# Two-layer streaming-encoder trunk on one core: second-matrix pairs with eight of sixteen row tiles in seven products, in single rotating rooms

## The chip, the cores and the metric

The kernel runs on one core of a Trainium2 chip. The core has a matrix engine (TensorE, in the profile PE, with its weight loads as PEld), a vector engine (DVE), a scalar engine (ACT), GpSimd (POOL) and SyncE (SP), which issues most of the DMA transfers. Each engine works through its own list of instructions in order and waits on semaphores for the others. The metric is the device time of one execution in microseconds, as the median of several runs.

## The reference

The input is a sequence of 256 rows of 2048 floats, batch 1. The model has two layers; what matters here are the two MLPs, one at the end of each layer:

```
def sq_relu_mlp(h, g, w1, w2):
    a = jax.nn.relu(rms_norm(h, g) @ w1)      # w1: 2048 x 8192
    return (a * a) @ w2                       # w2: 8192 x 2048

layer 1: h = h + attention_a(h) @ a_w_out;  h = h + sq_relu_mlp(h, ...)
shared:  k, v = split(rms_norm(h) @ kv_w)
layer 2: h = h + attention_b(h, k, v) @ b_w_out;  h = h + sq_relu_mlp(h, ...)
```

All values are float32. Both attentions have 16 heads of 128. The output is the 256 x 2048 result of the second layer.

## The kernel before, in words

**Products.** Every float32 operand is split into a high part `hi`, which the matrix engine can take at speed, and a low part `lo`, the remainder. A product is three passes (`passes`, lines 465 to 475): high by high, low activations by high weights, high activations by low weights. The activations are the stationary operand (128 x 128), the weights the moving one (128 x 512). The weights come from HBM; `issue` (lines 205 to 226) lets ACT copy a tile into `hi` (line 219) and DVE subtract to get `lo` (line 220). Each tile has 1024 columns, that is two blocks of 512. The `hi` and `lo` tiles have three buffers each, tiles of 512 columns (`hih`, `loh`) one.

**Pairs.** The output columns of a matrix are worked in panels of 512, two panels to a *pair*, a (first panel) and b (second). A pair has sixteen row tiles of 128 to sum over. A plain unit, written a4 or b7, takes two row tiles of one panel: 12 matmuls. Some of the row tiles go through seven products instead of eight (the Strassen-Winograd scheme on a 2 x 2 split of weights and rows). With weight blocks called 11, 12, 21 and 22, the sums T1 = 12 + 11, T3 = 22 + 12, T2 = T3 + 11 and T4 = T2 + 21 are made, and the seven *forms* use, in this order, 11, T3, T2, T1, 21, T4, 22 (numbers 0 to 6). The matching sums of activations are tiles `S` (from the normalised input) or `Sh` (from the hidden values), made by `sums` (lines 277 to 297). A plain pair has four row tiles in the seven products, a *wide* pair six: each of its forms has 1536 columns, a first half f of 1024 columns (6 matmuls) and a second half h of 512 (3 matmuls). After the second half of form 1, ACT copies an accumulator to the tile P7 (line 908) and puts a negated copy of another in its place (line 914); after that of form 2, DVE subtracts P7 (line 910); later line 918 adds it.

**The MLP.** The 8192 hidden columns are worked in four chunks c of 2048. Each chunk has two pairs of the first matrix, then two pairs of the second, which add to the residual stream. All second-matrix pairs (16 in the kernel, 8 in each MLP) and all but the first of the first-matrix pairs are wide. The hidden values of a chunk come in four quarters n of 512, one for each panel of the two first-matrix pairs. `turn_hidden` (lines 866 to 879) transposes a finished quarter in 32 x 32 blocks on DVE (line 331), carries it through HBM (`carry`: rows out at line 341, columns in at line 347) and then, in `take` (lines 842 to 864), applies relu (line 843), square into the high part (line 848), square (line 850) and the low part (line 854); the first two quarters also make `Sh`. Row tiles 8 to 11 are the third quarter (n = 2), 12 to 15 the fourth (n = 3).

**What sets the order.** `Pair.plan` (lines 130 to 142) writes the order of a pair's units by hand. A wide pair starts f0 h0 b5 f1 h1 b6 f2 h2 b7 f3 h3, where b5 to b7 are the last three units of the pair before; then its own a3 f4 h4 b3 f5 h5 a4 f6 h6 b4 a5 a6 a7. The loop in `mlp` (lines 898 to 930) takes the units one after another. For a plain unit `fetch` first calls `top_up`, which splits units ahead until three full ones are ready, and takes the first. A form's half is taken without topping up if one is ready; after a second half `top_up(AHEAD - 1)` splits until two full ones are ready, and the copy of line 908 stands ahead of that call. A ready tile with fewer than 1024 columns is not counted (line 233). After each plain unit `run_fill` takes one step off the list of side work (the steps of `carry` and `take` among it, at the numbers in `uses`, line 875). `keep_order` holds DVE, ACT, PE and SP to the order in which the program writes their instructions.

**Rooms.** The four blocks of a pair are loaded by SP (`bring`, line 811) into tiles with the tags `k` (blocks 11 and 22) and `v` (12 and 21), each with two buffers of 1536 columns. T3 is made by DVE (line 824) in a room called `bias`; T2 replaces T3 in place once T3 is split (line 224). T1 and T4 are made by POOL (`put`, line 830): a DMA that adds block 11 from HBM onto the room of 12, or block 21 onto the room of T2. `prepare` (lines 832 to 835) does this for the next pair when a given number of plain units is left before it, by the tuple `close = (7, 5, 1, 4, 3, 2)` for 12, 22, 21, 11, T3, T1.

Of the kernel before, what the change touches and what calls it, by code (L numbers as in the profile page):

```python
# [9 lines left out]
F32 = mybir.dt.float32  # L10
# [22 lines left out]
WIDE = UN + 512  # L33
WIDE1 = (1, 2, 3, 4, 5, 6, 7)
# [15 lines left out]
def trunk(ctx: ExitStack, tc: tile.TileContext, xT, xr, gs, hg, bf, wgate, w_in, w_oa, w1a, w1fa, w1sa, w2fa, w2sa,  # L50
# [24 lines left out]
    def load_x(i):  # L75
        raw_x[i] = qkv.tile([P, WIDE], F32, name="xin", tag="kv"[i // 2], bufs=2)[:, : GH * T].rearrange("p (a t) -> p a t", a=GH)
        if i:
            SY.dma_start(raw_x[i], xT[:, i * GH : (i + 1) * GH, :])
# [40 lines left out]
    class Pair:  # L119
# [3 lines left out]
        def __init__(self, big, src, order, third, units, wide=False):  # L123
            self.big, self.src, self.third, self.units, self.order = big, src, third, units, order
            self.ps, self.t, self.adds, self.wide, self.own = None, {}, order != "early", wide, 3 if wide else 2
# [4 lines left out]
        def plan(self, rest):  # L130
            made = [self.items(f"f{i} h{i}" if self.wide else f"f{i}") for i in range(7)]
            own = {"early": "a2 F a3 F b2 F b3 a4 b4 a5 a6 a7", "wide": "a3 F b3 F a4 F b4 a5 a6 a7", "ahead": "a3 F a4 F a5 F a6 a7 b3 b4",
                   "query": "a2 F b2 F a3 F b3 a4 b4 a5 a6 a7", "": "a2 F a3 F a4 F a5 a6 a7 b2 b3 b4"}[self.order].split()
            plan = made[0] + rest[:1] + made[1] + rest[1:2] + made[2] + rest[2:] + made[3]
            n = 4
            for i in own:
                if i == "F":
                    plan += made[n]
                    n += 1
                else:  # L140
                    plan += self.items(i)
            return plan, self.items("b5 b6 b7")

    def plan_mlp(w1, w1f, w1s, w2f, w2s, tail, more=None):
        pairs = []

        def add(w, wf, ws, i, wides, order, when):
            j = wides.index(i) if i in wides else i - sum(1 for k in wides if k < i)
            names = ("11", "12", "21", "22")
            if i in wides:  # L150
                src = [[None] * 3 + [ws[10 * j + 5 * q + u] for u in range(5)] for q in range(2)]
# [4 lines left out]
            pairs.append(Pair(big, src, order, len(pairs) % 2 == 0, when, i in wides))  # L156
# [48 lines left out]
    def issue(parts=1):  # L205
        form = None
        if not raws:
            load(parts)
        raw, cuts = raws.popleft()
        if not cuts:  # L210
            form, half = raw, raw.half
            raw, cuts = form.pair.t[form.name], [slice(0, 512 if half else UN)]
            if half:
                raw = raw[:, UN:]
        n = cuts[-1].stop
        hi = wsp.tile([P, n], F32R, name="hi" if n == UN else "hih", bufs=3 if n == UN else 1)
        lo = wsp.tile([P, n], F32R, name="lo" if n == UN else "loh", bufs=3 if n == UN else 1)
        for c in cuts:
            S.activation(hi[:, c], raw[:, c], AF.Copy)  # L219
            V.tensor_tensor(lo[:, c], raw[:, c], hi[:, c].bitcast(F32), op=ALU.subtract)  # L220
# [136 lines left out]
    def query_room(i):  # L357

        if not query:
            query.append(prob.tile([P, 9 * 3 * P], F32, name="query", tag="p", bufs=1))  # L360
        return query[0][:, i * UN : i * UN + UN]


    LONG = ((0, 0, 1, 3, 5, 6, 7, 8, 8), (0, 1, 2, 4, 6, 7), (0, 0, 1, 3, 5, 6), (0, 0, 1, 3, 5, 6))
# [133 lines left out]
    def form_products(ps, hi, lo, x, fs, i, half, stop):  # L498
        items = []
        for g in (2,) if half else range(2):  # L500
            if i in (0, 4, 5):
                xp = [x[2 * g + (i > 0)][:, k, (i == 5) * P : (i == 5) * P + P] for k in range(2)]
            else:
                c = {3: 0, 2: 1, 1: 2, 6: 3}[i]
                c = c * P if half else c * 256 + g * P
                xp = [fs[k + 2 * half][:, c : c + P] for k in range(2)]
            items.append((ps[i not in (4, 5)][i in (0, 5)], xp, g % 2, i < 2 and g == 0, i < 2 and g == stop))
# [87 lines left out]
    class Rooms:  # L595
# [3 lines left out]
        def open(self):  # L599
            self.t = prob.tile([P, 9 * 3 * P], F32, name="pbuf", tag="p", bufs=1)  # L600
            self.n = dict.fromkeys(self.at, 0)
# [174 lines left out]
    def decay_bias(g, box):  # L776
        nb = room("bias", "nb").rearrange("p (a t) -> p a t", a=GH)
# [12 lines left out]
    for g in range(NG):  # L790
# [12 lines left out]
        zk, k = turned(), room("k", "k")[:, : GH * T]  # L803
        v = room("v", "v")[:, :UN].rearrange("p (b c) -> p b c", b=NB)
# [8 lines left out]
    def make(p, name):  # L813
        t = p.t
        if name == "T3":
            if p.order in ("query", ""):
                t[name] = query_room(0)
            else:
                t[name] = prob.tile([P, 9 * 3 * P], F32, name="wT3", tag="p", bufs=1) if p.order == "early" else room("bias", "wT3")
# [3 lines left out]
        d, a, b = (t[i][:, : WIDE if p.wide else UN] for i in (name, a, b))  # L823
        V.tensor_tensor(d, a, b, op=ALU.add)

    def put(p, name):
# [3 lines left out]
        G.dma_start(p.t[name][:, : WIDE if p.wide else UN], p.big[other], accum_op=ALU.add)  # L830

    def prepare(p, d):
        for name, at in zip(("12", "22", "21", "11", "T3", "T1"), p.units):
            if d == at:
                (bring if name[0] != "T" else put if p.adds and name == "T1" else make)(p, name)

    def mlp(plan, x, Sx, st, last, more=None):
# [4 lines left out]
        def take(t, c, n):  # L842
# [16 lines left out]
            if n == 0:  # L859
                r = prob.tile([P, 9 * 3 * P], F32R, name="Sh", tag="p", bufs=1)  # L860
                Sh[c].extend(r[:, i : i + n] for i, n in ((0, UN), (UN, UN), (2 * UN, 512), (2 * UN + 512, 512)))
# [36 lines left out]
        for i, (p, q, u) in enumerate(plan):  # L898
# [5 lines left out]
            if q > 1:  # L904
                form_products(p.ps, hi, lo, p.x, p.fs, u, q == 3, 1 + p.wide)
# [5 lines left out]
                if q == 2 + p.wide:  # L911
                    top_up(AHEAD - 1)
                    if u == 1:
                        S.activation(p.ps[1][0], p.ps[1][1], AF.Copy, scale=-1.0)
            else:
# [49 lines left out]
    def rel_bias(g, box):  # L965
        rb = room("bias", "rb").rearrange("p (a t) -> p a t", a=GH)
# [11 lines left out]
    for g in range(NG):  # L978
        zk, k = turned(), room("k", "k")[:, : GH * T]
        v = room("v", "v")[:, :UN].rearrange("p (b c) -> p b c", b=NB)  # L980
# [30 lines left out]
def _wide(w):  # L1011

    import numpy as np
    c, n = w.shape[0] // D, w.shape[1] // 1024
    a = w.reshape(c, KT, P, n, 2, 512).transpose(0, 3, 4, 1, 2, 5)
    f = a[:, :, :, :6].reshape(c, n, 2, 3, 2, P, 512).transpose(0, 1, 4, 2, 5, 3, 6)
    s = a[:, :, :, 6:].reshape(c, n, 2, 5, 2, P, 512).transpose(0, 1, 2, 3, 5, 4, 6)
    return np.ascontiguousarray(f).reshape(-1, P, WIDE), np.ascontiguousarray(s).reshape(-1, P, UN)


def _pairs(w, wides):
# [3 lines left out]
    f, s = _wide(w)  # L1025
    f, s = f.reshape(-1, 4, P, WIDE), s.reshape(-1, 10, P, UN)
# [54 lines left out]
```

## Time and profile before

| what | us |
|---|---|
| median of 3 runs (2085.22 to 2088.07) | 2087.54 |
| the profiled execution: span from first to last instruction | 2084.3 |
| busy PE / DVE / ACT / POOL in that span | 2076.9 / 1629.7 / 1256.1 / 118.4 |
| one second-matrix pair, from 623.09 to 664.57 of the span | 41.48 |

The profile gives one execution, whose own time is its span; the median of the runs shown lies 3.2 us above it. Its parts are: busy time by engine; the span in 40 slices with the granted clock of the matrix engine (full speed in all 40); DMA queues; the chain of work that ended last, followed back from the last instruction; the costliest groups of instructions; and DMA issues with the time from issue to landing. A timeline row gives the start, the duration, the engine, the line of the kernel, the operation, the tiles written and read with their shapes, the count, and in brackets the engine's idle time before it with what ended it. Busy time is not a bound by itself: matmuls overlap, and an engine that is often idle can still be late at one place.

### The profile page before, as it was taken

Reading aid. Unit: us, or ns where it says so; the run is one execution under the profiler, and the core shown is the slowest. Engines: PE = TensorE matmul, PEld = TensorE weight load, DVE = VectorE, ACT = ScalarE, POOL = GpSimd, SP = SyncE. Lnnn points to the kernel's source line nnn. Section 1 sums busy time; section 2 is a strip of 40 time slices with the busy share of each in tenths; the row PEclk is TensorE's granted clock in tenths of the full one; section 3 lists DMA queues with packets and bytes.
Section 4 is the critical chain, followed back from the end, with each engine's and each line's share of the span. In section 5 each row is a group of like instructions: output and inputs, shape, how many; then the busy total and the mean of one; then the engine's idle time right before and its main releaser. Section 6 shows DMA issues by size and latency. Waiting matters only on the chain.

```text
span 2084.3 us, 26346 instructions
## 1 busy us (share of the span) xinstructions
PE 2076.9 (100%) x9230; PEld 1721.4 (83%) x9230; DVE 1629.7 (78%) x1964; ACT 1256.1 (60%) x1637; POOL 118.4 (6%) x131
## 2 busy tenths in 40 slices
PE   9999999999999999999999999999999999999999
PEld 7888888888888888888878888888888888888887
DVE  6767666888788888788888677778987887888786
ACT  6544455766566566567676455456765665665664
POOL 1111000000000000000011001000000000000000
PEclk9999999999999999999999999999999999999999
DMA  7787788798798799789988777787987987988895
GB/s 288 247 257 243 225 258 265 253 276 277 235 286 270 251 278 298 217 276 294 269 244 276 225 239 234 244 265 265 282 264 254 278 272 241 289 271 250 271 288 165
DMA packets 181397, 540.93 MB, mean 260 GB/s; under 512 B 36864, under 2 KB 71568, under 8 KB 181264
## 3 DMA queue, kind: packets, MB, share of 16 engines
q1 hardware_dynamic: 170384, 483.60, 68.7%
q0 software_dynamic: 10592, 55.08, 14.3%
q8 instruction: 72, 1.18, 0.2%
q10 hardware_dynamic: 288, 0.57, 0.1%
q14 instruction: 61, 0.50, 0.1%
HBM read 499.30 MB, written 39.87 MB: 259 GB/s over the span
## 4 chain that ended last, share of the span: by engine, by line
PE 98%; DMA 1%; DVE 0%; ACT 0%; issue 0%; ACTq 0%; DVEq 0%; SPq 0%
PE acc L473 26%; PE acc L471 26%; PE acc L475 26%; PE s L471 6%; PE s L473 6%; PE s L475 6%; PE s L614 1%; PE po L644 1%; DMA w<-in_w2fa 0%; PE s L613 0%; PE po L645 0%; DMA raw<-in_w_in 0%; DVE lo L220 0%; ACT hi L219 0%; PE s L737 0%
## 5 line engine op out<-in xcount | busy, mean ns | idle before, releaser
L220 DVE TENSOR_TENSOR lo<-raw,hi 128x1024 fp32r<-128x1024 f32 (+1 forms) x574 | 695.5, 1215 | 219.5 <-ACT hi L219 203.6
L219 ACT ACTIVATE hi<-raw 128x1024 fp32r<-128x1024 f32 (+1 forms) x574 | 602.8, 1051 | 255.6 <-PE acc L473 194.8
L471 PE MATMUL acc<-hi,act 128*128 128x512 f32 x2108 | 580.3, 393 | 1.6 <-ACT hi L219 1.6
L473 PE MATMUL acc<-hi,act 128*128 128x512 f32 x2108 | 571.3, 389 | 0.1
L475 PE MATMUL acc<-lo,act 128*128 128x512 f32 x2108 | 570.9, 389 | 0.0
L473 PEld LDWEIGHTS acc<-hi,act 128*128 128x128 f32 x2108 | 395.5, 188 | 83.2 <-DVE act L311 0.7
L475 PEld LDWEIGHTS acc<-lo,act 128*128 128x128 f32 x2108 | 395.6, 188 | 82.2
L471 PEld LDWEIGHTS acc<-hi,act 128*128 128x128 f32 x2108 | 393.7, 188 | 81.5 <-ACT hi L219 1.7
L219 ACT ACTIVATE hi<-w 128x1024 fp32r<-128x1024 f32 x138 | 145.7, 1056 | 108.1 <-DMA w<-in_w1fa 25.1
L220 DVE TENSOR_TENSOR lo<-w,hi 128x1024 fp32r<-128x1024 f32 x138 | 167.5, 1214 | 27.4 <-ACT hi L219 25.0
L220 DVE TENSOR_TENSOR lo<-wT,hi 128x1024 fp32r<-128x1024 f32 x94 | 114.6, 1219 | 64.0 <-ACT hi L219 64.0
L219 ACT ACTIVATE hih<-w 128x512 fp32r<-128x512 f32 x120 | 75.2, 627 | 76.5 <-PE acc L473 65.5
L219 ACT ACTIVATE hi<-wT 128x1024 fp32r<-128x1024 f32 x94 | 99.1, 1055 | 27.7 <-PE acc L473 9.1
L471 PE MATMUL s<-hi,act 128*128 128x512 f32 x386 | 104.6, 389 | 0.0
L475 PE MATMUL s<-lo,act 128*128 128x512 f32 x386 | 104.6, 389 | 0.0
L473 PE MATMUL s<-hi,act 128*128 128x512 f32 x386 | 104.6, 389 | 0.0
L219 ACT ACTIVATE hih<-wT 128x512 fp32r<-128x512 f32 x90 | 56.4, 627 | 72.9 <-PE acc L473 63.2
L220 DVE TENSOR_TENSOR loh<-w,hih 128x512 fp32r<-128x512 f32 x120 | 82.3, 686 | 18.9 <-ACT hih L219 18.8
L473 PEld LDWEIGHTS s<-hi,act 128*128 128x128 f32 x386 | 72.5, 188 | 15.1
L475 PEld LDWEIGHTS s<-lo,act 128*128 128x128 f32 x386 | 72.5, 188 | 15.0
L471 PEld LDWEIGHTS s<-hi,act 128*128 128x128 f32 x386 | 72.4, 188 | 15.0
L220 DVE TENSOR_TENSOR loh<-wT,hih 128x512 fp32r<-128x512 f32 x90 | 62.0, 689 | 21.0 <-ACT hih L219 20.7
(220 smaller groups left out, 1961.4 us busy)
## 6 DMA issues: line engine op xcount, KB each, us to landing
raw<-in_w_in SPq DMA_DIRECT2D x95, 512.0 KB, 4.5
raw<-in_w2sa SPq DMA_DIRECT2D x80, 512.0 KB, 5.8
raw<-in_w2sb SPq DMA_DIRECT2D x80, 512.0 KB, 5.8
raw<-in_w1sa SPq DMA_DIRECT2D x70, 512.0 KB, 6.0
raw<-in_w1sb SPq DMA_DIRECT2D x70, 512.0 KB, 6.0
raw<-in_w_kv SPq DMA_DIRECT2D x64, 512.0 KB, 4.5
turn<-z SPq DMA_DIRECT2D x60, 512.0 KB, 4.2
w<-in_w2fa SPq DMA_DIRECT2D x32, 768.0 KB, 7.4
```

Of the source, the lines that this page charges most:

```text
L219: S.activation(hi[:, c], raw[:, c], AF.Copy)
L220: V.tensor_tensor(lo[:, c], raw[:, c], hi[:, c].bitcast(F32), op=ALU.subtract)
L471: TE.matmul(ps[:, cols], xh, cut(hi, j), start=first, stop=False, **kw)
L473: TE.matmul(ps[:, cols], xl, cut(hi, j), start=False, stop=False, **kw)
L475: TE.matmul(ps[:, cols], xh, cut(lo, j), start=False, stop=last, **kw)
L614: TE.matmul(s[:, P : 3 * P], q[:, a, P:T], k[:, a], start=True, stop=True)
L644: TE.matmul(po[:, :T], v[:, 0, a * P : (a + 1) * P], pT[:, :2], start=True, stop=False)
```

## The change

The second-matrix pairs become *deep*: eight of the sixteen row tiles go through the seven products. Each form has 2048 columns, in two halves of 1024 (6 matmuls each), and eight plain units are left. The order of a deep pair's own units after h3 is a4 f4 h4 b4 f5 h5 a5 f6 h6 a6 a7. T3 is made in two halves, the first where T3 was made, the second one plain unit later; T2 is made in two halves, each after the matching half of T3 is split. The sums `Sh` of the second hidden quarter have twice the size. After each second half of a deep form `run_fill` is called as well, and the `uses` of the third and fourth quarters get other numbers.

The tags `k` and `v` with two buffers each become four tags `k0`, `k1`, `v0`, `v1` with one buffer each of 2048 columns, and so does `bias`. Which block goes to which tag rotates from pair to pair: 12 takes the room that 11 had, 22 that of 12, 11 that of 21, 21 that of 22. The tile of the pool `prob` grows from 3456 to 4096 columns, and the on-chip space for software DMA descriptors is set to 2048 bytes.

The diff, cut to its core (the host-side layout of the weights and the renaming of widths are left out):

```diff
+DEEP = 2 * UN
...
-        def __init__(self, big, src, order, third, units, wide=False):
+        def __init__(self, big, src, order, third, units, wide=UN):
...
+            self.deep, self.wide = wide == DEEP, wide > UN
+            self.cols, self.own = wide, wide // 512
...
-            own = {... "wide": "a3 F b3 F a4 F b4 a5 a6 a7", ...
+            own = {... "wide": "a3 F b3 F a4 F b4 a5 a6 a7", "deep": "a4 F b4 F a5 F a6 a7", ...
...
+        rooms = {"12": "v0", "22": "k0", "11": "k1", "21": "v1"}
...
-                add(None, w2f, w2s, i, WIDE2, "wide", close)
+                add(None, w2f, w2s, i, WIDE2, "deep", close, DEEP)
...
         for p in pairs:
+            p.rooms = rooms
+            if p.adds:
+                rooms = {"12": rooms["11"], "22": rooms["12"], "11": rooms["21"], "21": rooms["22"]}
...
-            raw, cuts = form.pair.t[form.name], [slice(0, 512 if half else UN)]
+            raw, cuts = form.pair.t[form.name], [slice(0, form.pair.cols - UN if half else UN)]
...
-        if form and half == form.pair.wide:
+        if form and form.pair.deep and form.name == "T3":
+            make(form.pair, "T2", int(half))
+        elif form and half == form.pair.wide:
...
     def half_next():
         u = raws[0][0] if raws else units[0]
-        return isinstance(u, Form) and u.half
+        return isinstance(u, Form) and u.half and not u.pair.deep
...
-        return qkv.tile([P, WIDE], dtype, name=name, tag=tag, bufs=1 if tag == "bias" else 2)
+        return qkv.tile([P, DEEP], dtype, name=name, tag=tag, bufs=1)
...
-    LONG = ((0, 0, 1, 3, 5, 6, 7, 8, 8), (0, 1, 2, 4, 6, 7), ...
+    LONG = ((0, 0, 1, 3, 10, 11, 12, 13, 13), (0, 1, 2, 4, 8, 9), ...
...
-        for g in (2,) if half else range(2):
+        groups = p.cols // 512
+        for g in range(2, groups) if half else range(2):
...
-        p.t[name] = room("kv"[name in ("12", "21")], "w" + name)
-        SY.dma_start(p.t[name][:, : WIDE if p.wide else UN], p.big[name])
+        p.t[name] = room(p.rooms[name], "w" + name)
+        SY.dma_start(p.t[name][:, : p.cols], p.big[name])
...
-        d, a, b = (t[i][:, : WIDE if p.wide else UN] for i in (name, a, b))
+        cols = slice(0, p.cols) if half is None else slice(half * UN, min(half * UN + UN, p.cols))
+        d, a, b = (t[i][:, cols] for i in (name, a, b))
...
-        G.dma_start(p.t[name][:, : WIDE if p.wide else UN], p.big[other], accum_op=ALU.add)
+        G.dma_start(p.t[name][:, : p.cols], p.big[other], accum_op=ALU.add)
...
     def prepare(p, d):
+        if p.deep and d == p.units[4] - 1:
+            make(p, "T3", 1)
         for name, at in zip(("12", "22", "21", "11", "T3", "T1"), p.units):
-            if d == at:
+            if d == at and p.deep and name == "T3":
+                make(p, "T3", 0)
+            elif d == at:
                 (bring if name[0] != "T" else put if p.adds and name == "T1" else make)(p, name)
...
             elif n == 1:
-                yield from sums([[t3[:, 2 * j + b : 2 * j + b + 1] for j in range(2)] for b in range(NB)], Sh[c][2:], 1)
+                yield from sums([[t3[:, 2 * j + b :: 4] for j in range(2)] for b in range(NB)], Sh[c][2:])
...
-                    uses = ((4, 5, 6, 7, 8, 9, 9), (4, 5, 5, 5, 6, 7, 7), (4, 5, 6, 7), (4, 4, 5, 5))[n]
+                    uses = ((4, 5, 6, 7, 8, 9, 9), (4, 5, 5, 5, 6, 7, 7), (6, 7, 8, 9), (6, 6, 7, 7))[n]
+                    wait = int(n == 3)
...
-                    add_fill(carry(*zt, 0)[:2] + [[step] * uses.count(i) for i in range(3, uses[-1] + 1)])
+                    add_fill(carry(*zt, wait)[: 2 + wait] + [[step] * uses.count(i) for i in range(3 + wait, uses[-1] + 1)])
...
                 if q == 2 + p.wide:
                     top_up(AHEAD - 1)
                     if u == 1:
                         S.activation(p.ps[1][0], p.ps[1][1], AF.Copy, scale=-1.0)
+                    if p.deep:
+                        run_fill()
...
-    nc = bacc.Bacc("TRN2", target_bir_lowering=False, num_devices=1)
+    nc = bacc.Bacc("TRN2", target_bir_lowering=False, num_devices=1, dynamic_dma_scratch_size=2048)
```

More of the change, by code (lines that the diff above doesn't have):

```diff
@@ L121, in trunk @@
         fast = True
-        def __init__(self, big, src, order, third, units, wide=False):
-            self.big, self.src, self.third, self.units, self.order = big, src, third, units, order
-            self.ps, self.t, self.adds, self.wide, self.own = None, {}, order != "early", wide, 3 if wide else 2
+        def __init__(self, big, src, order, third, units, wide=UN):
+            self.big, self.src, self.third, self.units = big, src, third, units
+            self.ps, self.t, self.adds, self.order = None, {}, order != "early", order
+            self.deep, self.wide = wide == DEEP, wide > UN
+            self.cols, self.own = wide, wide // 512
         def items(self, names):
@@ L145, in plan_mlp, with add @@
         pairs = []
-        def add(w, wf, ws, i, wides, order, when):
+        def add(w, wf, ws, i, wides, order, when, cols=WIDE):
             j = wides.index(i) if i in wides else i - sum(1 for k in wides if k < i)
@@ L155, in add @@
                 big = {k: src[int(k[1]) - 1][int(k[0]) - 1] for k in names}
-            pairs.append(Pair(big, src, order, len(pairs) % 2 == 0, when, i in wides))
+            pairs.append(Pair(big, src, order, len(pairs) % 2 == 0, when, cols if i in wides else UN))
         close = (7, 5, 1, 4, 3, 2)
+        rooms = {"12": "v0", "22": "k0", "11": "k1", "21": "v1"}
         for c in range(NCH):
@@ L504, in form_products @@
                 c = {3: 0, 2: 1, 1: 2, 6: 3}[i]
-                c = c * P if half else c * 256 + g * P
+                c = c * P if half and not p.deep else c * 256 + g % 2 * P
                 xp = [fs[k + 2 * half][:, c : c + P] for k in range(2)]
-            items.append((ps[i not in (4, 5)][i in (0, 5)], xp, g % 2, i < 2 and g == 0, i < 2 and g == stop))
+            items.append((ps[i not in (4, 5)][i in (0, 5)], xp, g % 2, i < 2 and g == 0, i < 2 and g == groups - 1))
         passes(items, hi, lo, skip_group_check=True)
@@ L818, in make @@
             else:
-                t[name] = prob.tile([P, 9 * 3 * P], F32, name="wT3", tag="p", bufs=1) if p.order == "early" else room("bias", "wT3")
+                t[name] = prob.tile([P, 4 * UN], F32, name="wT3", tag="p", bufs=1) if p.order == "early" else room("bias", "wT3")
         else:
@@ L904, in mlp @@
             if q > 1:
[L905 removed]
+                form_products(p.ps, hi, lo, p.x, p.fs, u, q == 3, p)
                 if u == 1 and q == 2 + p.wide:
```

56 lines of the change are left out of this document (30 added, 26 removed).

## The prediction

> **What bounds the kernel now.** I read the engines' shares first, then the chain that ended last, then the windows of the changed stage, then the timelines of one pair.
>
> ```profile
> span 2084.3 us, 26346 instructions
> ...
> PE 2076.9 (100%) x9230; PEld 1721.4 (83%) x9230; DVE 1629.7 (78%) x1964; ACT 1256.1 (60%) x1637; POOL 118.4 (6%) x131
> ...
> PE 98%; DMA 1%; DVE 0%; ACT 0%; issue 0%; ACTq 0%; DVEq 0%; SPq 0%
> ```
>
> TensorE sets the end: 98% of the chain. The next rows are two windows, the two second-matrix pairs of one column chunk (I call them pair 0 and pair 1).
>
> ```profile
> 623.09:664.57 41.48, 41.48 (x184) 34.36 (x183) 35.52 (x39) 29.32 (x35) 1.71 (x2) 1.00 1.00 303
> 664.57:706.05 41.48, 41.48 (x184) 34.36 (x183) 31.09 (x32) 22.81 (x28) 1.71 (x2) 1.00 0.77 239
> ```
>
> Columns: busy us of PE, PEld, DVE, ACT, POOL, then granted clock, DMA share, GB/s. A pair's plan has 7 first halves of 6 matmuls, 7 second halves of 3 and 10 units of 12: 183. 41.48 / 183 = 0.2267 us each, without a hole, although DVE is only 75 to 86% busy. So matmuls removed here are time gained, if the engines that feed PE keep the order that hides them. I write f0 to f6 and h0 to h6 for a form's halves, a4, b7 and so on for plain units; a pair starts f0 h0 b5 f1 h1 b6 f2 h2 b7 f3 h3.
>
> **What is removed.** A deep pair has 14 halves of 6 matmuls and 8 units of 12: 180. Three fewer in 16 pairs: 48 x 0.2267 = **-10.9 us**.
>
> **What is moved: the units behind the halves.** `top_up` counts a tile shorter than 1024 columns as nothing. A wide second half was such a tile, so two full units stood ready behind it. A deep second half is full: `fetch` at b5 stops at b5, f1, h1, and when h1 has been taken nothing is left. b6 is then split after h1's products, in ACT's written order after the copy P7 (line 908), which waits for h1 on PE. Before, b6's split came first (first row, line 219; it ends 626.69):
>
> ```profile
> 625.64 1.05 ACT L219 ACTIVATE hi<-raw 128x1024 fp32r<-128x1024 f32 x1
> 630.09 0.60 ACT L908 ACTIVATE p<-s 128x512 f32<-128x512 f32 x1 [3.40 <-PE s L475]
> 630.59 1.05 ACT L219 ACTIVATE hi<-wT 128x1024 fp32r<-128x1024 f32 x1
> 631.53 0.59 ACT L914 ACTIVATE s<-s 128x512 f32<-128x512 f32 x1
> ```
>
> ```profile
> 629.66 0.39 PE L475 MATMUL s<-loh,Sh 128*128 128x512 f32 x1
> 629.89 1.07 PE L471 MATMUL acc<-hi,act 128*128 128x512 f32 x4
> 630.80 1.07 PE L473 MATMUL acc<-hi,act 128*128 128x512 f32 x4
> 631.71 1.07 PE L475 MATMUL acc<-lo,act 128*128 128x512 f32 x4
> 632.61 0.62 PE L471 MATMUL s<-hi,Sh 128*128 128x512 f32 x2
> ```
>
> 629.66 is h1's last matmul, 629.89 b6's first, 632.61 f2's first: b6 hides the chain from P7 to f2, whose `hi` is ready at 631.64, only 0.97 us before it is wanted. In the changed kernel the split at 630.59 is b6's own. PE, free at 629.89, stands until 631.64, plus about 0.03 for the signal: 1.78 us. Queued behind P7 on ACT are both splits and the copy of line 914. **16 x 1.78 = +28.5 us.**
>
> **The same drain on DVE after h2.** Line 910 waits for h2; the low part of b7, before it in the order until now, comes after it.
>
> ```profile
> 634.42 0.39 PE L475 MATMUL s<-loh,Sh 128*128 128x512 f32 x1
> 634.65 1.07 PE L471 MATMUL acc<-hi,act 128*128 128x512 f32 x4
> ```
>
> ```profile
> 633.65 1.23 DVE L220 TENSOR_TENSOR lo<-raw,hi 128x1024 fp32r<-128x1024 f32 x1 [0.15 <-ACT hi L219]
> 634.85 0.70 DVE L910 SCALAR_TENSOR_TENSOR acc<-s,p 128x512 f32<-128x512 f32 x1
> 635.54 1.23 DVE L220 TENSOR_TENSOR lo<-w,hi 128x1024 fp32r<-128x1024 f32 x1
> 638.42 1.31 DVE L331 STREAM_TRANSPOSE z<-acc 128x512 f32<-128x512 f32 x2
> 639.65 1.18 DVE L220 TENSOR_TENSOR lo<-w,hi 128x1024 fp32r<-128x1024 f32 x1
> 646.90 1.22 DVE L854 TENSOR_TENSOR act<-q,act 128x1024 fp32r<-128x1024 f32 x1
> 648.04 1.22 DVE L220 TENSOR_TENSOR lo<-w,hi 128x1024 fp32r<-128x1024 f32 x1
> ```
>
> Line 910 starts 0.20 after h2 (634.85 against 634.65) and hands over after 0.69. b7's low part then ends at 0.20 + 0.69 + 1.22 + 0.03 = 2.14, and b7's third pass wants it at 8 x 0.2267 = 1.81: 0.33 in every pair. In pair 0 the queue goes on: low parts of f3 and h3, the two transposes of the last hidden quarter, low parts of a4 and f4, and behind them line 854 for the third hidden quarter, which `run_fill` at h3 now puts directly ahead of a4, its first reader. Full operations follow each other at 1.14 (646.90 to 648.04), the transposes take 1.23 (638.42 to 639.65). From h2's end: 0.20 + 0.69 + 3 x 1.14 + 1.23 + 2 x 1.14 + 1.22 + 0.03 = 9.07. PE asks for it in a4's second pass: b7 2.72, f3 and h3 2.72, first pass 0.91, in all 6.35. Wait 2.72, with the 0.33 in it. In pair 1 line 592 stands for the transposes and nothing of line 854: no more than the 0.33. **8 x 2.72 + 8 x 0.33 = +24.4 us** (ends: 16 x 0.33 = 5.3 if the queue has a hole for line 854, and 24.4).
>
> **The fourth hidden quarter, pair 0.** Its steps move to a5 and h6; a6 reads it.
>
> ```profile
> 652.56 0.61 PE L475 MATMUL s<-lo,Sh 128*128 128x512 f32 x2
> ```
>
> ```profile
> 652.76 1.06 ACT L219 ACTIVATE hi<-raw 128x1024 fp32r<-128x1024 f32 x1 [0.75 <-PE s L473]
> 653.73 1.04 ACT L843 ACTIVATE q<-q 128x1024 f32<-128x1024 f32 x1
> ```
>
> With three `hi` buffers a split starts 0.20 after the second pass of the unit three places before (652.76 against 652.56). Line 854 is written behind the splits of a6 and a7, and a7 waits for f6. From a5's start: f6's second pass ends at 2.72 + 0.91 = 3.63; a7's `hi` ends at 3.83 + 1.05 = 4.88, its low part hands over 1.17 later, line 854 ends at 7.27 + 0.03. a6's second pass would come at 2.72 + 2 x 1.36 + 0.91 = 6.35. 0.95 late: **8 x 0.95 = +7.6 us** (ends 0 and 7.6).
>
> **The start of pair 0.** T3 becomes two halves, the second ahead of h0's low part, and the sums of lines 286 to 289 double.
>
> ```profile
> 619.53 1.06 ACT L219 ACTIVATE hi<-w 128x1024 fp32r<-128x1024 f32 x1 [2.16 <-DMA w<-in_w2fa]
> ```
>
> ```profile
> 610.18 0.42 DVE L286 TENSOR_TENSOR sum<-q 128x256 f32<-128x256 f32 x1
> 611.65 2.35 DVE L220 TENSOR_TENSOR lo<-raw,hi 128x1024 fp32r<-128x1024 f32 x2
> 613.92 1.28 DVE L296 TENSOR_TENSOR Sh<-sum,Sh 128x512 fp32r<-128x512 f32 x2
> 619.78 1.71 DVE L824 TENSOR_TENSOR wT<-w,w 128x1536 f32<-128x1536 f32 x1
> 621.42 1.21 DVE L220 TENSOR_TENSOR lo<-w,hi 128x1024 fp32r<-128x1024 f32 x1
> ```
>
> ```profile
> raw<-in_w2sa SPq DMA_DIRECT2D x80, 512.0 KB, 5.8
> w<-in_w2fa SPq DMA_DIRECT2D x32, 768.0 KB, 7.4
> wT<-in_w2fa POOLq DMA_DIRECT2D x8, 768.0 KB, 7.5
> w<-in_w2fa POOLq DMA_DIRECT2D x8, 768.0 KB, 8.9
> ```
>
> DVE's run from f0's low part to h1's: f0 1.14, four sums 1.47 (610.18 to 611.65), T3's second half 1.14, h0 1.14, two lines 296 1.28, b5 and f1 2.28, T2's first half 1.14, h1 1.22: 10.8 us. PE wants the end at 623.09 + 3 x 1.36 + 2.72 + 0.91 = 630.80. With a T3 half of 1.14 for the 1.64 of 619.78, DVE is free at 620.9: ends 631.7, 0.9 late. But f0's `hi` waits at 619.53 for a load that grows from 768 to 1024 KB: by the rows at 512 and 768, 1.6 us more. Then f0's low part starts at 619.53 + 1.6 + 1.06 = 622.2 and the run ends 2.2 late. I take 1.6: **8 x 1.6 = +12.8 us** (ends 7 and 18).
>
> **Costed at nothing.** The accumulates T4 and T1 grow to 1 MB, by the same step some 9 and 11 us; T4 is asked for after eight units (h2 to b4, 5 x 1.36 + 3 x 2.72 = 15 us), T1 after 19; if that cover goes, ACT's `hi` waits for the DMA and each us costs PE 16. A pair moves 10 MB for 9.5; the DMA share is 1.00 in pair 0, but the waits stretch that window. The free order of the four rooms lets loads start earlier; no matmul here waits for a room, so nothing is gained. No row shows a smaller descriptor scratch (2048 bytes): 0, else as T4's delay.
>
> **Sum.** -10.9 + 28.5 + 24.4 + 7.6 + 12.8 = +62.4. The profiled span 2084.3 becomes 2146.7; the median, 3.2 us above that span, 2087.5 + 62.4 = **2149.9 us**, 3.0% slower.
>
> **The rivals.**
> 1. *Faster.* If b6's split stands before P7 on ACT, as at 625.64, and the low parts likewise, PE never waits and the gain is kept: 2076.6. The point that decides is whether a fourth unit is ready at h1. For it: DVE's 25% of idle time. Against: the written order, which idle time does not change. Chance 0.10.
> 2. *Only the two copies' waits*, 28.5 and 16 x 0.33, because these very waits let DVE catch up elsewhere: -10.9 + 33.8, 2110.4. For it: DVE idles while PE waits; against: the queue behind line 910 starts after that idle time. Chance 0.25.
> 3. *Transfers late too.* The share of 1.00 says pair 0's window is near full; T1 or T4 2 us late in each pair adds 32: 2182. Against: 15 us of cover. Chance 0.10.
> 4. *The clock falls* at the waits. PE's idle time before its first real matmul left it alone:
>
> ```profile
> 7.20 0.73 PE L471 MATMUL acc<-hi,act 128*128 128x512 f32 x2 [1.55 <-ACT hi L219]
> ```
>
> The clock is 1.00 in every window, and 1.55 us did not change that; waits up to 2.7 are not shown. If one 2.72 us unit ran at half speed after each P7 wait, 16 x 2.72 = 43.5 more: 2193. Chance 0.03. The Trainium skill ("TensorE: Matmul & The Clock Gate", HAM oscillation) puts the gap that throttles at about 3.4 us, by which nothing is added, and the row of 1.55 agrees; its section on psum-queue depth-cycling says that frequent short idling throttles too, which would be this rival.
>
> My forecast has 0.52: 2150, its own bounds 2123 (line 854 on time everywhere: 8 x 2.39 + 7.6 less) to 2155 (the start 2.2 late). The range takes in rival 2 and some of rival 3: 2105 to 2172, about 8 in 10. 0.2% (4 us) is about what a measurement of this kernel can tell from no change: faster 0.10, same 0.02, slower 0.88.
>
> **What would show it.** PE holes of 1.8 us before the first matmul of a unit behind each h1 with ACT's line 908 in front of its `hi`; in pair 0 a hole inside a4 ended by line 854; matmuls 9182. No hole at all, or holes ended by DMA, would prove me wrong.

## The result, and the profile after

The changed kernel takes 2174.26 us (2172.68 to 2184.92) against 2087.14 for the kernel before beside it: a ratio of 1.0425, interval 1.0407 to 1.0442. It is 87.1 us slower; I had forecast 62.4 more, with an upper end of 2172. The profiled execution is the slowest of the six, 2184.92 where the others lie between 2172.68 and 2177.02, so its count of what the clock does, below, is that of a slow one.

The page of the kernel after, in the rows that answer to those of before:

```profile
span 2183.1 us, 26253 instructions
...
PE 2105.0 (96%) x9182; PEld 1719.0 (79%) x9182; DVE 1683.2 (77%) x1972; ACT 1287.5 (59%) x1613; POOL 117.9 (5%) x131
...
PE 3%; ACT 0%; issue 0%; DVE 0%; DVEq 0%; ACTq 0%
...
w<-in_w2fa SPq DMA_DIRECT2D x32, 1024.0 KB, 7.9
```

9182 matmuls are the 48 fewer that were forecast. The chain's shares add up to 3%: it was followed back only a little way, so nothing can be read from it, and the windows and timelines have to do. The two pairs of one chunk in the kernel after (PE, PEld, DVE, ACT, POOL busy, granted clock, DMA share, GB/s):

```profile
458.95:510.03 51.08, 44.33 (x182) 34.39 (x180) 41.24 (x42) 31.96 (x35) 2.53 (x3) 0.97 0.86 270
510.03:553.21 43.18, 41.45 (x181) 33.63 (x180) 34.62 (x33) 25.05 (x27) 1.72 (x2) 1.00 0.70 200
```

180 matmuls need 40.8 us. Pair 1 lost 2.4 and pair 0 lost 10.3, where the forecast had 2.1 (1.78 + 0.33) and 7.1 (1.78 + 2.72 + 0.95 + 1.6). Some 1.7 of pair 0's 10.3 is the clock, shown below. The DMA share did not rise to the limit: 0.86, less than the 1.00 of before. Pair 0's timeline shows where; TensorE first:

```profile
463.45 0.73 PE L485 MATMUL s<-lo,act 128*128 128x512 f32 x2 [2.04 <-DVE lo L228]
469.32 0.73 PE L485 MATMUL s<-lo,Sh 128*128 128x512 f32 x2
471.69 1.47 PE L481 MATMUL acc<-hi,act 128*128 128x512 f32 x4 [1.63 <-ACT hi L227]
487.85 1.20 PE L483 MATMUL acc<-hi,act 128*128 128x512 f32 x4 [2.04 <-DVE act L872]
```

The idle time in brackets runs from the modelled end of a matmul; a matmul's slot is shorter. h1's last two start at 469.32, so b6 could have started at 469.32 + 2 x 0.2267 = 469.77 and started at 471.69: 1.91 lost where the bracket has 1.63. I add these 0.28 to each bracket: the third pass of h0 (463.45) lost 2.3, the second of a4 (487.85) also 2.3. What ACT and DVE did meanwhile:

```profile
457.34 2.01 ACT L227 ACTIVATE hi<-w 128x1024 fp32r<-128x1024 f32 x2 [3.81 <-DMA w<-in_w2fa]
470.09 0.60 ACT L927 ACTIVATE p<-s 128x512 f32<-128x512 f32 x1 [5.46 <-PE s L485]
470.59 1.05 ACT L227 ACTIVATE hi<-raw 128x1024 fp32r<-128x1024 f32 x1
```

```profile
458.43 1.23 DVE L228 TENSOR_TENSOR lo<-w,hi 128x1024 fp32r<-128x1024 f32 x1 [1.31 <-ACT hi L227]
459.58 0.42 DVE L296 TENSOR_TENSOR sum<-q 128x256 f32<-128x256 f32 x1
...
461.04 1.22 DVE L838 TENSOR_TENSOR wT<-w,w 128x1024 f32<-128x1024 f32 x1
462.18 1.22 DVE L228 TENSOR_TENSOR lo<-w,hi 128x1024 fp32r<-128x1024 f32 x1
...
479.10 0.70 DVE L929 SCALAR_TENSOR_TENSOR acc<-s,p 128x512 f32<-128x512 f32 x1 [3.80 <-PE s L485]
479.71 1.22 DVE L228 TENSOR_TENSOR lo<-raw,hi 128x1024 fp32r<-128x1024 f32 x1
480.84 2.36 DVE L228 TENSOR_TENSOR lo<-w,hi 128x1024 fp32r<-128x1024 f32 x2
483.11 1.31 DVE L341 STREAM_TRANSPOSE z<-acc 128x512 f32<-128x512 f32 x2
484.34 1.19 DVE L228 TENSOR_TENSOR lo<-raw,hi 128x1024 fp32r<-128x1024 f32 x1
485.45 1.22 DVE L228 TENSOR_TENSOR lo<-w,hi 128x1024 fp32r<-128x1024 f32 x1
486.58 1.22 DVE L872 TENSOR_TENSOR act<-q,act 128x1024 fp32r<-128x1024 f32 x1
```

Line numbers have moved: 219 is now 227, 220 is 228, 471 to 475 are 481 to 485, 854 is 872, 908 is 927, 910 is 929. The copy P7 stands ahead of b6's `hi` on ACT (470.09, 470.59). The copy of form 2, the low parts of b7, f3 and h3, the transposes, the low parts of a4 and f4 and then line 872 follow each other on DVE without a gap, as written down beforehand.

One thing in the windows was not forecast, the granted clock (last but two):

```profile
469.01:472.42 3.41, 1.73 (x7) 0.94 (x6) 2.24 (x3) 2.33 (x3) 0.00 (x0) 1.00 1.05 249
472.42:475.84 3.42, 3.42 (x9) 2.69 (x9) 2.83 (x3) 3.42 (x5) 0.25 (x1) 0.50 0.99 345
475.84:479.25 3.41, 3.41 (x16) 2.76 (x16) 0.15 (x1) 2.11 (x4) 0.61 (x1) 1.00 1.07 358
```

The window behind the wait runs at half speed, 9 matmuls where the next has 16, and then the clock is whole again. In this execution it happened 10 times in the second-matrix pairs and once at the start of the kernel.

### The profile page after: what moved, and what is told of

Read it like the earlier page. It is cut to its first block, busy times and chain, and to the rows that moved or that the text cites. A ratio compares the mean times of both kernels' runs of the same rounds, so it can differ in the third digit from the quotient of the medians.

```text
span 2183.1 us, 26253 instructions
## 1 busy us (share of the span) xinstructions
PE 2105.0 (96%) x9182; PEld 1719.0 (79%) x9182; DVE 1683.2 (77%) x1972; ACT 1287.5 (59%) x1613; POOL 117.9 (5%) x131
## 5 line engine op out<-in xcount | busy, mean ns | idle before, releaser
L228 DVE TENSOR_TENSOR lo<-raw,hi 128x1024 fp32r<-128x1024 f32 (+1 forms) x542 | 655.3, 1214 | 238.8 <-ACT hi L227 227.6
L227 ACT ACTIVATE hi<-raw 128x1024 fp32r<-128x1024 f32 (+1 forms) x542 | 570.4, 1054 | 321.9 <-PE acc L483 253.8
L483 PE MATMUL acc<-hi,act 128*128 128x512 f32 x2092 | 579.9, 394 | 23.4 <-DVE act L872 23.3
L481 PE MATMUL acc<-hi,act 128*128 128x512 f32 x2092 | 584.4, 396 | 14.9 <-ACT hi L227 14.9
L227 ACT ACTIVATE hi<-w 128x1024 fp32r<-128x1024 f32 x202 | 212.9, 1058 | 123.8 <-PE acc L483 58.9
L228 DVE TENSOR_TENSOR lo<-w,hi 128x1024 fp32r<-128x1024 f32 x202 | 244.2, 1219 | 30.2 <-ACT hi L227 26.4
L228 DVE TENSOR_TENSOR lo<-wT,hi 128x1024 fp32r<-128x1024 f32 x142 | 173.4, 1222 | 52.0 <-ACT hi L227 49.6
L227 ACT ACTIVATE hi<-wT 128x1024 fp32r<-128x1024 f32 x142 | 149.1, 1055 | 56.5 <-PE acc L483 46.7
L838 DVE TENSOR_TENSOR wT<-wT,w 128x1024 f32<-128x1024 f32 (+1 forms) x48 | 66.3, 1381 | 1.6
L838 DVE TENSOR_TENSOR wT<-w,w 128x1024 f32<-128x1024 f32 (+1 forms) x48 | 65.5, 1364 | 0.0
L567 POOL TENSOR_TENSOR ss<-ss,mhalf 128x4 f32<-128x4 f32 x32 | 43.6, 1371 | 271.7 <-DVE ss L566 271.6
```

The costliest lines, as they stand in the source:

```text
L481: TE.matmul(ps[:, cols], xh, cut(hi, j), start=first, stop=False, **kw)
L483: TE.matmul(ps[:, cols], xl, cut(hi, j), start=False, stop=False, **kw)
L567: G.tensor_tensor(rn, vv, mhalf, op=ALU.pow)
```

## The experiments

Two theories. **Q** (queue): the waits come from the order in which ACT's and DVE's work is written, as in the prediction. **L** (load): the deep pairs ask more of DVE, ACT or the transfers than fits, and the waits only show where. Unless another is named, an edit is made to the kernel after.

**e9: only the order, no deep pair.** The kernel before, with a short tile counted like a full one, so that a wide pair gets the order of a deep one.

```diff
-        ready.append((hi, lo, n < UN))
+        ready.append((hi, lo, False))
```

> The kernel before, with the one difference that a ready second half counts as a full unit, so that its queue drains as in the changed kernel; the work stays that of before. Theory Q: 30 wide pairs wait 1.9 us behind h1 and some 0.3 behind h2, 2087 plus 57 to 70, some 2150 us. Theory L: 2087 to 2095 us.

Measured 2167.39, ratio 1.0378 (1.0362 to 1.0393). The waits of TensorE in this run (us in total, times, longest):

```profile
PE s L471 <- ACT hi L219: 26.1, 16, 1.6
PE acc L471 <- ACT hi L219: 25.7, 19, 1.6
```

With the old blocks, rooms and loads the wait behind h1 stands at 1.91 again (1.63 in the bracket), in all 30 wide pairs of both matrices, and 0.37 behind h2. These are 30 x 2.28 = 68 of the 80 us that this one word in `issue` costs; the rest are smaller waits that Q's 2150 did not have. The order alone makes the first two waits.

**e1: b6 split ahead of P7.**

```diff
+                if p.deep and q == 2:
+                    top_up(AHEAD - 1)
                 if q == 2 + p.wide:
```

> The changed kernel, but after each first half of a deep form one more unit is split, so that a plain unit stands ready behind every second half again. If the drained queue is the cause (theory Q): the 1.9 us waits behind h1 (16 of them) and the 0.37 us waits behind h2 go, the wait inside a4 of pair 0 shrinks by about 1.1, the clock hardly falls any more, and the waits at h0 and a6 of pair 0 stay: 2174 less 31, 6, 9 and about 10, some 2118 us. If the added work of DVE, ACT and DMA is the cause (theory L, the order being of no matter): the waits come back at other places, over 2155 us.

Measured 2132.41, ratio 1.022 (1.0204 to 1.0235). The waits behind h1 and h2 are gone in all 16 pairs, which is Q. The 2118 of Q was missed by 14, 9 of it since a4's wait did not shrink with them. TensorE's waits in pair 0 of this run:

```profile
463.15 0.73 PE L485 MATMUL s<-lo,act 128*128 128x512 f32 x2 [2.08 <-DVE lo L228]
484.05 1.21 PE L483 MATMUL acc<-hi,act 128*128 128x512 f32 x4 [2.33 <-DVE act L872]
```

**e4: the fill ahead of the splits**, so that line 872 stands earlier on DVE.

```diff
+                if p.deep and q == 3:
+                    run_fill()
                 if q == 2 + p.wide:
...
-                    if p.deep:
-                        run_fill()
```

> The changed kernel with the side work of a second half ahead of the two splits instead of behind them. Theory Q: the low part of the hidden values (line 872) then stands in front of the low parts of a4 and f4 (a6 and a7), and the waits inside a4 (2.3 us) and a6 (1.15 us) of pair 0 go: 2174 less 8 x 3.4 = 27, some 2147 us. Theory L: DVE has the same work, the wait moves to the next third pass, less than 8 us gained.

Measured 2146.64, ratio 1.0288 (1.0268 to 1.0308), as Q said: of a4's wait 0.2 is left and nothing of a6's; the waits of h0 and b6 stay.

**e5: the edits of e1 and e4 together.**

> The two edits of e1 and e4 together: a unit ready behind every half, and the side work ahead of the splits. Theory Q: only the wait at the start of pair 0 is left (2.0 to 2.6 us, 8 times) and the clock stays up: 2087 less 10.9 plus 16 to 21, some 2094 us. Theory L: over 2115 us.

Measured 2119.48, ratio 1.0157 (1.0141 to 1.0172): together the edits gain 55 of the 69 that their two gains add up to, and Q's 2094 was missed. TensorE's waits in pair 0; pair 1 has none:

```profile
461.33 0.72 PE L485 MATMUL s<-lo,act 128*128 128x512 f32 x2 [2.05 <-DVE lo L228]
480.68 1.20 PE L483 MATMUL acc<-hi,act 128*128 128x512 f32 x4 [0.83 <-DVE act L872]
498.62 1.19 PE L483 MATMUL acc<-hi,act 128*128 128x512 f32 x4 [1.20 <-DVE act L872]
```

So in pair 0 taking one wait away lets another take part of its place.

**e3: TensorE kept busy behind h1** by six matmuls that nobody reads.

```diff
+                if p.deep and (q, u) == (3, 1):
+                    idle = ps_o.tile([P, 512], F32, name="pt", tag="po")
+                    for _ in range(6):
+                        TE.matmul(idle, p.fs[2][:, :P], hi[:, :512], start=True, stop=True)
```

> The changed kernel with six extra matmuls of 512 columns (1.36 us) into an unused accumulator behind h1 of each deep pair, inside the wait of 1.9 us for the copy P7. If the fall of the clock is a cost of its own (theory K): the clock stays at full speed in most of the pairs, every wait keeps its length to the end of it, and the time falls by 8 to 14 us, to some 2162. If the clock does not matter: 2174 or a little more.

Measured 2170.85, ratio 1.0407 (1.039 to 1.0425): 3.4 less than after, where 12 were expected, and the two intervals overlap. The clock still fell, three times in the profiled execution, each time at a4's wait, which had no spare work.

**e8: spare matmuls in pair 0's other waits as well**: beside e3's, eight ahead of h0, eight ahead of a4 and four ahead of a6, 256 in all.

```diff
+            if p in pairs and p.deep and pairs.index(p) % 4 == 2:
+                spare = {(3, 0): 8, (0, 4): 8, (0, 6): 4}.get((q, u), 0)
+            if spare:
...
+                for _ in range(spare):
+                    TE.matmul(idle, p.x[0][:, 0, :P], hi[:, :512], start=True, stop=True)
```

> The changed kernel with 256 extra matmuls into an unused accumulator, laid into its waits: 6 behind h1 of every deep pair, and in pair 0 8 ahead of h0, 8 ahead of a4, 4 ahead of a6. They add 58 us of work to PE and compute nothing. Theory K (PE's idle time makes the clock fall, and that costs time of its own): the clock stays at full speed, the time falls by 10 to 14 us to some 2162. If the falls of the clock cost nothing: 2174 or more.

Measured 2163.39, ratio 1.0365 (1.0349 to 1.038). Its page:

```profile
span 2159.9 us, 26766 instructions
...
PE 2143.3 (99%) x9438; PEld 1756.1 (81%) x9438; DVE 1682.4 (78%) x1972; ACT 1285.8 (60%) x1613; POOL 119.1 (6%) x131
```

256 matmuls more, 58 us of TensorE's time, and the kernel is 10.9 us faster than after: the clock is whole in all four runs. The waits are as long as in the kernel after: at a4 the eight spare matmuls take 1.81 of the 2.31, and 0.46 to 0.50 is left in every pair 0. So I put the 10.9 down to the clock.

**e2: rooms alone.** The rooms of 2048 columns, their rotation, the larger `prob` tile and the smaller descriptor space, with the pairs left wide (and `uses` and the sums as before).

```diff
-                add(None, w2f, w2s, i, WIDE2, "deep", close, DEEP)
+                add(None, w2f, w2s, i, WIDE2, "wide", close)
```

> Only the rooms, their rotation, the larger tile of the pool prob and the small descriptor space, with the wide pairs of the kernel before. Theories Q and L: these cost nothing, 2087 us within 4. If single rooms hold loads back or the descriptor space makes the accumulating transfers wait (theory R): over 2100 us, with ACT's splits waiting for DMA.

Measured 2088.52, ratio 1.0005 (0.9996 to 1.0014). The rooms, their rotation and the descriptor space cost nothing here; the transfers in this run are still those of 768 KB.

**e6: pair 0's start earlier** (on e5): 22, 11 and T3 one plain unit sooner.

```diff
-                add(None, w2f, w2s, i, WIDE2, "deep", close, DEEP)
+                add(None, w2f, w2s, i, WIDE2, "deep", close if q else (7, 6, 1, 5, 4, 2), DEEP)
```

> e5, and for pair 0 of each chunk the loads of the blocks 22 and 11 and the two halves of T3 one plain unit earlier. If the start of pair 0 is late because f0 waits for a larger load and because a half of T3 stands behind f0 (theory S): that wait falls from 2.6 to under 1 us, 2076 to 2085 us, faster than before. If DVE has simply too much work from there on (theory L): the wait stays at 2 us or more, no better than e5.

Measured 2119.35, ratio 1.0152 (1.0129 to 1.0176): the wait of h0 fell to 1.2 or less, and the time stayed. a4 kept its wait of 1.1, a6 waits 0.8 to 1.5 with a new wait for ACT's `hi` of 0.5 to 1.5 just ahead of it in five of the eight chunks, and the clock fell twice in the profiled execution. What holds a6 in this run is a transfer: ACT's relu waits for the fourth quarter's way through HBM in all eight chunks (0.6 to 2.9 us), and DVE stands idle behind it. TensorE, ACT and DVE in the first chunk:

```profile
498.34 1.19 PE L483 MATMUL acc<-hi,act 128*128 128x512 f32 x4 [1.08 <-DVE act L872]
```

```profile
492.79 1.06 ACT L861 ACTIVATE q<-q 128x1024 f32<-128x1024 f32 x1 [1.23 <-DMA q<-turn]
```

```profile
495.92 1.23 DVE L228 TENSOR_TENSOR lo<-raw,hi 128x1024 fp32r<-128x1024 f32 x1 [1.98 <-ACT hi L227]
```

DVE in this run from 446 to 480, ahead of that:

```profile
446.00:480.00 34.00, 32.54 (x139) 25.26 (x137) 32.27 (x39) 25.01 (x29) 1.69 (x2) 1.00 0.92 298
```

32.27 of 34: this looked like L, for the first part of pair 0 alone. So I changed DVE's work itself.

**e14 and e15: less and more work for DVE** (on e6). In each chunk e14 leaves out two low parts of the second quarter's sums (`skip` is set there), and e15 forms them twice.

```diff
-        for i in range(n):
+        for i in range(0 if skip else n):
             V.tensor_tensor(lo[i], w[i], hi[i].bitcast(F32), op=ALU.subtract)
```

```diff
+        for i in range(n if skip else 0):
+            V.tensor_tensor(wk.tile([P, 512], F32, name="sum", tag="wk"), w[i], hi[i].bitcast(F32), op=ALU.subtract)
```

> e6_early with 1.28 us less work for VectorE in each column chunk: the low part of the sums over the second quarter is not formed, and the passes read the first quarter's in its place (so the sums' low part is wrong for one quarter of the rows; the time alone is read). If what is left in pair 0 is VectorE's supply, e6_early's 2119 should fall by about 8 x 1.28 = 10 us to 2109. If the written order or the transfers hold it, nothing changes: 2116 to 2122.

> e6_early with 1.28 us more work for VectorE in each column chunk: the two subtractions of the low parts of the sums are done a second time into a tile that nobody reads. If VectorE's supply is what is left in pair 0: about 10 us more, 2129. If the written order or the transfers hold it: 2116 to 2122.

Measured 2120.28, ratio 1.0161 (1.0145 to 1.0177), and 2117.11, ratio 1.014 (1.0123 to 1.0157). Neither followed DVE's load; L falls as a sum. The traces say why. In e14 DVE has pauses in the same stretch:

```profile
461.17 1.22 DVE L228 TENSOR_TENSOR lo<-raw,hi 128x1024 fp32r<-128x1024 f32 x1 [0.51 <-ACT hi L227]
468.57 1.23 DVE L228 TENSOR_TENSOR lo<-wT,hi 128x1024 fp32r<-128x1024 f32 x1 [0.24 <-ACT hi L227]
470.03 1.23 DVE L228 TENSOR_TENSOR lo<-wT,hi 128x1024 fp32r<-128x1024 f32 x1 [0.23 <-ACT hi L227]
471.92 1.23 DVE L228 TENSOR_TENSOR lo<-raw,hi 128x1024 fp32r<-128x1024 f32 x1 [0.67 <-ACT hi L227]
```

These pauses, 1.65 in all, are ended by ACT's `hi`; e6 has two of them, 0.24 and 0.67, so 0.74 of the 1.28 us came back as pauses. What makes h0 late stands ahead of the place where work was taken out or added: its wait in this chunk is 1.20 in e6, 1.23 in e14 and 1.22 in e15. In e15 the added work does hold TensorE up at once, at b5, the second row (the first is h0's wait):

```profile
461.29 0.73 PE L487 MATMUL s<-lo,act 128*128 128x512 f32 x2 [0.95 <-DVE lo L228]
464.84 1.20 PE L487 MATMUL acc<-lo,act 128*128 128x512 f32 x4 [0.97 <-DVE lo L228]
```

b5's wait of 1.24 is new, 8 x 1.24 = 9.9. But later waits became smaller: those for line 872 (874 in e15) went from 19.2 us in e6 to 15.0 in all, and those for ACT's `hi` ahead of a6, 4.6 in e6, are gone. The clock was whole in all four runs of e15 and between 0.997 and 1.000 in e6's. So DVE binds at the start of pair 0. a4's wait stays between 1.0 and 1.2 in all three runs, whatever DVE has to do, and a6's hangs on the transfer: ACT's relu waits for the fourth quarter 14.2 us in all in e6, 18.0 in e14 and 6.0 in e15, so a good part of what DVE's work gives or takes at the start of a pair is evened out there.

**e7: the third quarter's steps one unit earlier** (on e6), with pair 1's block 22 one sooner.

```diff
-                    uses = (... (6, 7, 8, 9), (6, 6, 7, 7))[n]
+                    uses = (... (5, 6, 7, 8), (6, 6, 7, 7))[n]
```

> e6, and in pair 0 the steps of the third hidden quarter one side-work slot earlier (line 872 ahead of the two transposes), and for pair 1 block 22 loaded one plain unit earlier. If line 872's place is what is left of the wait inside a4 (theory Q): that wait of 1.1 us goes, 8 x 1.1 = 9 less, and the wait inside a6 becomes 0.5 us longer or stays: some 2110 to 2115 us. If DVE has too much work in the 34 us that it runs here without a pause (theory L): the 1.1 us come back at the third pass of a4 or f4, 2119 us.

Measured 2127.47, ratio 1.0192 (1.0177 to 1.0207), 8 slower than e6. The wait inside a4 is gone, as Q said, with 0.5 left at its third pass, but other waits came. Waits of the whole run, ACT's and then TensorE's (us in total, times, longest):

```profile
ACT q L861 <- DMA q<-turn: 19.4, 17, 3.4
```

```profile
PE s L481 <- ACT s L937: 5.7, 8, 1.2
```

The first row was 19.2 us in 10 times in e6, most of it at the fourth quarter; new are waits of 0.3 to 0.9 at the third quarter's relu, in six of the eight chunks. That relu now stands between P7 and the negated copy, and the copy is late for f2's first pass, once in each of the 8 pairs: earlier in the order is not earlier in the data.

**e11: the low parts of the `Sh` sums on GpSimd** (on e7).

```diff
-            V.tensor_tensor(lo[i], w[i], hi[i].bitcast(F32), op=ALU.subtract)
+            (G if side else V).tensor_tensor(lo[i], w[i], hi[i].bitcast(F32), op=ALU.subtract)
```

> e7, with the low parts of the sums Sh of the first two hidden quarters (line 306, 1.28 us for two) on POOL instead of DVE. Theory L (DVE's work binds at the start of pair 0): the waits at h0 and h1 fall by about 1.2 us in each pair 0, 10 us less than e7. Theory Q: no change beyond 3 us. If POOL is slow with them and f1 waits for it: longer than e7, with a hole before f1's matmuls.

Measured 2126.17, ratio 1.0189 (1.0172 to 1.0206), the same as e7. That does not speak against L: DVE lost 2.57 us of work a chunk and got slower beside GpSimd. GpSimd, then DVE, in this run:

```profile
458.71 4.45 POOL L306 TENSOR_TENSOR Sh<-sum,Sh 128x512 fp32r<-128x512 f32 x2 [1.53 <-ACT Sh L303]
```

```profile
460.27 1.73 DVE L228 TENSOR_TENSOR lo<-raw,hi 128x1024 fp32r<-128x1024 f32 x1 [0.51 <-ACT hi L227]
461.92 2.32 DVE L228 TENSOR_TENSOR lo<-wT,hi 128x1024 fp32r<-128x1024 f32 x1
```

Two low parts of 1.22 took 1.73 and 2.32 while GpSimd ran, 1.61 more, where 1.28 had been taken off DVE.

**e12 and e13: only pair 1 deep**, pair 0 wide as before; e12 with e5's order, e13 with the order of the change.

```diff
-                add(None, w2f, w2s, i, WIDE2, "deep", close, DEEP)
+                if q:
+                    add(None, w2g, w2h, i, DEEP2, "deep", close, DEEP)
+                else:
+                    add(None, w2f, w2s, i, WIDE2, "wide", close)
```

> Only pair 1 of each chunk is deep, with the two order edits of e5; pair 0 stays wide as before (with the full sums of the second hidden quarter). What is left in e5 lies in pair 0 alone, where DVE runs without a pause for some 34 us. If that is so (theory L, for pair 0 only): 8 x 3 matmuls less, 5.4 us, and no new wait above 1 us: 2080 to 2085 us, faster than before. If deep pairs cost wherever they stand: 2090 us or more.

> As e12, but without the order edits: pair 1 deep as in the changed kernel. Theory Q: eight waits of 1.9 us behind h1 and eight of 0.37 behind h2, 18 us more than e12, some 2100 us, and no fall of the clock, since a wait of 1.9 us alone did not make it fall. Theory L: as e12.

Measured 2093.77, ratio 1.0033 (1.002 to 1.0045), and 2116.05, ratio 1.0147 (1.013 to 1.0165). The order is worth 22 us in 8 pairs: 8 x (1.91 + 0.37) = 18, and the clock, which fell three times in the pairs of e13's profiled execution where Q had it whole. e12 has 24 matmuls fewer (5.4 us) and still does not reach the kernel before, nor the 2080 to 2085 of L: its profile has some 10 us of waits more than before's, 5.8 of them at the starts of deep pairs. No version beat the kernel before.

## Why the prediction was wrong

The direction, the places and the order as their cause held. Two steps failed: the start of pair 0 was mis-sized, 12.8 for 21.0 us, and the clock was put at nothing where it cost 10.9. By its steps:

| step | predicted | measured in the kernel after |
|---|---|---|
| matmuls removed | -10.9 | -10.9 |
| P7, behind h1 | +28.5 | 16 x 1.91 = 30.6 |
| drain after h2: b7, a4 | +24.4 | 16 x 0.37 + 8 x 2.31 = 24.4 |
| fourth hidden quarter, a6 | +7.6 | 8 x 1.15 = 9.2 |
| start of pair 0 | +12.8 | 8 x (2.31 + 0.32) = 21.0 |
| the clock | 0 | 10.9 (after less e8) |
| sum | +62.4 | 85.2, of 87.1 |

The waits are those of the profiled execution, the mean over the chunks (h1's 0.32 in six of the eight); the clock's row and the 87.1 are from the medians. The span of the profiled execution lies 98.8 above before's; its granted clock was 0.991, that of the other five 0.993 to 0.995. Outside the table, TensorE waits 2.4 us in the first pair behind layer 1's MLP.

**The start of pair 0** was mis-sized by 8.2. The run of DVE's work was right: from f0's low part (458.43) to h0's (462.18) it took 3.75, which is the prediction's 1.14 + 1.47 + 1.14. The load was not. By the prediction's rows the run ended 0.9 late without it and 2.2 late with it; it took 1.6. In the kernel after ACT begins f0's `hi` 1.61 ahead of the pair's first matmul (457.34, 458.95), where the row of before has 3.56 (619.53, 623.09): 1.95 later, where the step of the load was 1.6. So the 2.2 were lost in full, and 0.4 more: 2.31 at h0 and 0.32 at h1. The prediction also laid the whole wait at h1, though by its own rows h0's low part was already 1.8 late: 622.2 + 1.14 + 1.47 + 1.14 + 1.22 = 627.2, against 623.09 + 1.36 + 0.91 = 625.36. e6, which brings the load and both halves of T3 earlier, cut h0's wait to 1.2 or less. In this chunk 1.3 of the 1.95 is a later issue by SP (450.46 against 613.27, each from the pair's first matmul) and 0.6 a longer way; why it was issued later is open.

**The clock,** rival 4, had 0.03 and happened beside the forecast, not in its place. The sum put it at nothing on one row, a wait of 1.55 that did no harm, though the sum itself held waits of up to 2.72. That row was close to the edge: at the same place the kernel after waited 1.83, and the window behind it ran at half clock.

```profile
7.38 0.73 PE L481 MATMUL acc<-hi,act 128*128 128x512 f32 x2 [1.83 <-ACT hi L227]
```

Of the ten falls in the pairs, five stand behind a4's wait, two behind h0's, and three behind the 1.91 after h1 together with h1's own 0.32. Half a window is lost each time, 1.7 us. In pair 1 of the kernel after, with 1.91 alone, it never happened.

**Rival 1** is refuted by ACT's rows at 470; **rival 2** by the kernel after itself, where h0, a4 and a6 wait beside the two copies. **Rival 3** is not what happened: no wait of TensorE is ended by a DMA, and the share is below before's. But the load at the pair's start is a transfer that came late by way of ACT, which it did not name; in one chunk f0 itself waited 1.5 us for it.

**Costed at nothing:** rooms, rotation and descriptor space are at nothing (e2); T1 and T4 hold nothing up in the second-matrix pairs of the kernel after.

Not settled: how the 32 us that e5 still lies above the kernel before divide among DVE's supply at the pair's start, a4's place in the order, the fourth quarter's way through HBM ahead of a6 and the clock. e6, e7, e11, e14 and e15 each moved one of them, and the others took up most of it.

## What to carry to other kernels

Before a tile's size changes, look for the code that counts tiles by size: here a test for "short" kept one more unit ready, and without it the same kernel loses 80 us. Where work runs in a fixed order, hold every end in a run against its own demand, and take a late load at what its rows say, not at a middle value. When the sum itself holds waits longer than any that a row shows to be harmless, give the clock a price; and add up waits that lie near each other before calling each too short.

## What the runs showed of the hardware

**The clock falls on the sum of idle time.** Two windows and the ones behind them, from the kernel after (a4's wait of 2.31, then pair 1's 1.91):

```profile
1015.15:1018.56 3.41, 1.37 (x7) 0.82 (x6) 3.41 (x4) 0.77 (x1) 0.00 (x0) 1.00 0.98 347
1018.56:1021.97 3.41, 3.41 (x10) 2.67 (x9) 1.50 (x3) 1.06 (x1) 0.00 (x0) 0.50 0.97 363
516.80:520.21 3.41, 1.78 (x8) 1.17 (x7) 0.56 (x2) 1.82 (x3) 0.00 (x0) 1.00 0.59 221
520.21:523.62 3.41, 3.41 (x16) 2.76 (x16) 3.34 (x3) 3.08 (x4) 0.00 (x0) 1.00 0.43 161
```

Counted in slots of 0.2267, TensorE is idle for 2.3 us of the first and 1.8 of the third. In the MLPs of the runs here, every window of 3.41 us with 2.2 us of idle TensorE or more was followed by one at half clock, and none with less than 1.9; between, both occurred. e9's 30 waits of 1.9, each alone, brought no fall; in e13 three of the same waits did, each with another of 0.33 or more in its window. The Trainium skill ("TensorE: Matmul & The Clock Gate", HAM oscillation) warns of idle gaps over about 3.4 us; here a little over 2 us, in one piece or in two, did it, and the measurement decides. Matmuls that nobody reads won 10.9 us (e8).

**GpSimd beside DVE.** A subtraction of 128 x 512 takes GpSimd 2.15 us on average (e11) and DVE 0.68 (before), and DVE's own of 128 x 1024 went from 1.22 to 1.73 and 2.32 meanwhile. The Trainium skill ("SBUF — State Buffer", Who interferes with whom) says that GpSimd's ports are DVE's second pair and are locked; these rows agree.
